# A two-layer streaming encoder: the first weight pieces taken tile by tile, another order of the first transfers, cache rows written from loaded tiles, and new keys

## The chip, the core and the metric

The kernel runs on one core of a Trainium2 chip, as one program. The metric is the device time of one execution in microseconds (us). The core has the engines PE (matmul; its weight loads are shown as PEld), DVE (VectorE), ACT (ScalarE), POOL (GpSimd) and SP, whose queue issues all transfers of this kernel. The transfers run on 16 DMA engines. Each engine takes its instructions in order; they wait for each other through semaphores.

## The reference

Two layers are computed over 1152 rows: 1024 frames of one new stream (eight tiles of 128 rows, tiles 0 to 7) and 16 frames of each of eight running streams (tile 8). All is in float32.

```python
xn = rms_norm(x, norm_mix)
q, k, v, u = split(xn @ w_in)                       # 512 | 128 | 128 | 512 columns
q, k = rope(rms_norm(q, q_gain)), rope(rms_norm(k, k_gain))
attn = sink_attention(q, keys, vals, sinks)         # 128 rows of window, 8 heads on 2 kv heads
pool = multi_scale_pool(u) @ w_pool * scale
x = x + concat(attn, pool) @ w_out                  # 1024 x 1024
h = rms_norm(x, norm_ffn) @ w_up                    # 1024 x 5632
c = conv_b + sum(h[t - 2 + j] * conv_w[j] for j in range(3))
x = x + (silu(c_gate) * c_val) @ w_down             # 2816 x 1024
```

For the running streams, keys and values are those of a cache of 128 rows followed by the 16 new ones. The newest 128 rows of keys and values are outputs: for these streams, rows 16 to 127 of the cache (outputs `nk_s` and `nv_s`, rows 0 to 111) and the 16 new rows.

## The kernel before

**Products.** A float32 product is made of three matmuls (`mm3`, lines 153 to 156) on operands that are split into a rounded part and the rest. A weight piece is loaded as 128 x 512 floats into a tile `raw` (five of them), and `w_split` makes the rounded part with a cast (line 182 on DVE, line 184 on ACT; the key `e_w` says how many of four consecutive pieces go to DVE) and the rest with a subtract (line 185, DVE), into a tile `W` (six of them, 512 KB each). The mixer goes through its weights three times, for three batches of three tiles. A piece with a key is stored after its split into DRAM (`wsd`, line 188; the profile calls these arrays wd0k, wd0u, wd0o and so on), and later batches load it from there (line 179) and don't split again. `w_advance` loads up to five pieces ahead and splits up to three ahead of the unit that is being written.

**A mixer layer.** For batch b, the stream `n` has the norms: for each tile `normA` (square and sum on ACT, line 255; a small scale on DVE, 256; the power on POOL, 257; the product with the gain on DVE, 258) and `normB` (eight transposes on PE, 278, a cast on ACT, 281, and a subtract on DVE, 282). `k0` to `k2` are the projections for q, k and v: eight pieces of 512 columns (one block of 128 rows each) and four of 256 columns (two blocks each), every one with three tiles. `u0` to `u2` make the pooling input, `p` the pooling product, `L` the attention of each tile step by step, `o` the output projection. `m0` to `m2` are the norms for the FFN.

**The hand-over to the FFN.** The FFN's up-projection uses seven products of sums (a Strassen-like scheme): `s0` and `s1` are twelve steps each, five splits (lines 314 on ACT and 315 on DVE), four additions (line 323) and others, for the first and the second half of the rows. `v` and `w` are the seven products of the first column pair for these halves; their results leave PSUM through ACT copies (line 932) or DVE additions (line 927). PSUM has four tiles `mm`, two `s` and two `tr`. The down-projection is also made of seven products, with five or four units each; `wt_load` fetches five and a half blocks of w_down that several products share, and `wd_load` the others.

**What sets the order.** The streams of a mixer layer are lists of tokens. A token has a key from `PLAN` (start and step for each stream, in no unit), tokens that must stand before it, and a few counts of buffers. `arrange` takes, again and again, the token of the smallest key that is allowed. This gives the order in which the program is written. From it the framework makes the order of each engine: it takes instructions by this order as a priority, but by its own model of time, so that instructions whose inputs are ready may pass others. Keys that begin with `e_` say which of ACT (0) or DVE (1) does a copy: `e_q`, `e_k`, `e_v` for the projections' results, `e_u` for the pooling input, `e_k2` for the keys, `e_pt0` and `e_pt1` for the transposed attention weights.

**The beginning.** `start` (lines 1328 to 1336) issues the first transfers: tile 0 of x, the identity, piece 0, the gain (a row broadcast to 128 partitions, 512 KB), piece 1, tiles 1 and 2, the other constants. In layer 0 the first norms are written as A, A, A, B, B, B (`wide` in `norms`), and `k0` follows when all three tiles are normed. `copies` (lines 1338 to 1342) moves the cache's rows 16 to 127 from DRAM to the outputs in DRAM, two transfers for each layer. `sample` loads the same caches into SBUF (lines 668 and 672) for the attention of tile 8.

Of the kernel before, what the change touches and what calls it, by code (L numbers as in the profile page):

```python
# [44 lines left out]
def arrange(tokens, limits):  # L45
# [19 lines left out]
PLAN = [  # L65
    dict(k0=(-17.62, 0.24), u0=(10.61, 1.71), k1=(30.79, 2.26), u1=(78.0, 4.62), o0=(92.76, 2.89), k2=(148.67, 0.53), u2=(167.09, 2.77), o1=(177.0, 4.18), o2=(235.82, 4.28), p0=(40.1, 4.11), p1=(87.53, 9.52), p2=(194.05, 11.9), n1=(-17.77, 3.16), n2=(24.42, 3.62), n3=(92.75, 0.67), m0=(218.99, 3.57), m1=(259.62, 0.1), m2=(181.18, 1.22), d=(4.13, 4.36), L=(26.9, 49.72, 64.52, 85.1, 108.8, 144.29, 159.45, 183.94, 209.44, 245.41), cw=(276.93, 6.24), sc=(242.61, 32.45), s0=(252.65, 2.67), s1=(279.21, 6.7), v=(236.08, 0.18), w=(265.61, 1.32), upw=(297.57, 0.58), e_q=0, e_k=1, e_v=1, e_u=0, e_k2=0, e_qt=0, e_pt0=0, e_pt1=1, e_ps0=1, e_ps1=1, e_ks=0, e_w=1, e_x0=0, e_x1=0, e_x2=1),
    dict(k0=(-52.3, 0.11), u0=(39.12, 0.62), k1=(27.74, 4.1), u1=(77.36, 4.61), o0=(81.16, 2.69), k2=(144.54, 0.53), u2=(154.52, 4.44), o1=(176.58, 5.19), o2=(244.07, 2.25), p0=(50.25, 5.11), p1=(72.82, 0.77), p2=(195.1, 13.29), n1=(-13.38, 2.12), n2=(30.2, 4.39), n3=(93.86, 2.01), m0=(219.6, 1.94), m1=(237.49, 1.8), m2=(278.02, 1.14), d=(-26.81, 5.35), L=(26.9, 49.72, 64.52, 87.91, 107.72, 142.58, 160.43, 180.13, 216.19, 239.71), cw=(266.26, 12.19), sc=(271.63, 4.65), s0=(264.1, 2.05), s1=(266.18, 3.7), v=(283.58, 0.14), w=(284.07, 11.47), upw=(287.29, 0.87), e_q=1, e_k=1, e_v=0, e_u=1, e_k2=0, e_qt=0, e_pt0=0, e_pt1=0, e_ps0=1, e_ps1=1, e_ks=0, e_w=1, e_x0=0, e_x1=1, e_x2=0),
]
# [3 lines left out]
def encoder_kernel(ctx: ExitStack, tc: tile.TileContext, consts, x_prompt, x_sample, cache_k, cache_v,  # L72
# [260 lines left out]
    def kvq_units(l, b):  # L333
        us = []
        for c, (cols, kn, n) in enumerate(((0, 1, 512), (512, 2, 256))):
            hold = {}
            for j in range(8 // kn):
                def f(w, c=c, kn=kn, n=n, j=j, hold=hold):
                    xT = state["xT", b]
                    wh, wl = [v.rearrange("p (k n) -> p k n", k=kn) for v in (w.hi, w.lo)]  # L340
                    for tl in range(3):
                        t = b * 3 + tl
                        if j == 0:
                            hold[tl] = P("mm")
                        o = hold[tl][:, 0:n]
# [4 lines left out]
                        if (j + 1) * kn == 8:  # L350
                            if c == 0:
                                state["qkv", t] = T("B", [128, 640])
                                copy(l, "e_q", state["qkv", t][:, 0:512], o)
                            else:
                                state["V", t] = T("V", [128, 128])
                                copy(l, "e_k", state["qkv", t][:, 512:640], o[:, 0:128])
                                copy(l, "e_v", state["V", t], o[:, 128:256])
                us.append(Unit(f, [in_piece(w_in[l], kn * j, cols, kn, n)]))
        return us
# [301 lines left out]
    def sample(l):  # L661
# [536 lines left out]
    def down_units(l):  # L1198
        us = []
        for u, (j, p) in enumerate(DSEQ):  # L1200
# [4 lines left out]
            def f(u=u, j=j, p=p, n=n, late=late, loads=loads, splits=splits):  # L1205
# [39 lines left out]
    def params1(l):  # L1245
        def f():
# [91 lines left out]
    def copies(l):  # L1338
        def f():
            sync.dma_start(out=nk_s[l, :, 0:112], in_=cache_k[l, :, 16:128])  # L1340
            sync.dma_start(out=nv_s[l, :, 0:112], in_=cache_v[l, :, 16:128])
        return f

    events = []
    pend = []
    for l in range(DEPTH):
# [160 lines left out]
```

## Time and profile before

| what | us |
|---|---|
| median of 3 runs | 2243.28 |
| lowest and highest | 2240.95, 2246.43 |
| the profiled execution | 2242.44 |
| its span, first to last instruction | 2240.7 |
| PE busy | 2169.5 (97%) |
| DVE busy | 1712.6 (76%) |
| ACT busy | 943.5 (42%) |

The mixer of layer 0 and its hand-over fill roughly the first 448 us, the FFN goes on to about 1120, the mixer of layer 1 and its hand-over to about 1520, and its FFN to the end. The mean granted clock of PE is 0.988. A row of a timeline has the start, the duration, the engine, the line, the operation with the tile it writes and the tiles it reads, and in brackets the idle time before it and what ended that. Busy time of PE counts matmuls up to modelled ends, so a busy PE can still run at a lower clock; the column with the granted clock shows that.

### The profile page before, as it was taken

The page shows a single profiled execution, that of the slowest core. Times are in us where ns is not written, and L with a number is a line of the kernel's source. Part 1 is how long each engine was busy: PE and PEld are TensorE (multiplying, and loading weights), DVE is VectorE, ACT ScalarE, POOL GpSimd, SP SyncE. Part 2 cuts the span into 40 slices and gives each one's busy share as a digit, 9 for nine tenths or more (in the row PEclk, how much of TensorE's full clock was granted, in tenths as well). Part 3 has the DMA queues.
Part 4 walks back from the last instruction along what each step waited for, and adds up shares of the span by engine and source line. Part 5 has one row for each costly group of instructions (what it writes and reads, how often), then busy time and mean ns, then how long its engine had stood idle before and what let it go on. Part 6 is the DMA issues. An engine that isn't in the chain of part 4 may idle for free.

```text
span 2240.7 us, 36002 instructions
## 1 busy us (share of the span) xinstructions
PE 2169.5 (97%) x13178; PEld 1945.5 (87%) x13178; DVE 1712.6 (76%) x3234; ACT 943.5 (42%) x1749; POOL 326.6 (15%) x499
## 2 busy tenths in 40 slices
PE   7999999899999999999999999979999999999999
PEld 6867777899999999878888887779999999988887
DVE  4776467989899998867557754689989999987663
ACT  3454345534343434443335543554343434353341
POOL 0000001121213232000000000111212233320000
PEclk9999999899999999999999999999999999999999
DMA  8757565122224346958765665532222343488663
GB/s 313 255 194 269 182 218 173 59 95 79 95 88 151 117 151 220 298 178 268 243 228 184 230 230 207 205 116 84 94 82 93 110 140 128 143 274 267 182 199 113
DMA packets 315940, 389.64 MB, mean 174 GB/s; under 512 B 21906, under 2 KB 219746, under 8 KB 315730
## 3 DMA queue, kind: packets, MB, share of 16 engines
q1 hardware_dynamic: 315762, 387.33, 52.2%
q8 instruction: 104, 1.70, 0.3%
q14 instruction: 74, 0.61, 0.1%
HBM read 279.71 MB, written 109.37 MB: 174 GB/s over the span
## 4 chain that ended last, share of the span: by engine, by line
PE 85%; DMA 6%; DVE 5%; ACT 2%; issue 1%; SPq 0%; POOL 0%; DVEq 0%; ACTq 0%
PE mm L154 15%; PE mm L155 15%; PE mm L156 15%; PE s L156 11%; PE s L154 11%; PE s L155 11%; PE s L644 2%; DMA raw<-in_w_down_dram 1%; DMA raw<-in_w_in_dram 1%; PE tr L631 1%; PE mm L448 1%; DMA W<-wd1o 1%; PE s L592 1%; DMA xd<-u 1%; PE tr L294 1%
## 5 line engine op out<-in xcount | busy, mean ns | idle before, releaser
L154 PE MATMUL mm<-B,W 128*128 128x288 f32 (+1 forms) x1376 | 422.1, 307 | 13.6 <-DVE B L927 7.7
L155 PE MATMUL mm<-B,W 128*128 128x288 f32 (+1 forms) x1376 | 419.2, 305 | 1.9 <-DVE B L315 1.8
L156 PE MATMUL mm<-B,W 128*128 128x288 f32 (+1 forms) x1376 | 417.2, 304 | 0.0
L154 PE MATMUL s<-B,B 128*128 128x512 f32 x704 | 279.6, 397 | 4.1 <-ACT B L1133 2.7
L156 PE MATMUL s<-B,B 128*128 128x512 f32 x704 | 279.2, 397 | 2.8 <-DVE B L1134 2.8
L155 PE MATMUL s<-B,B 128*128 128x512 f32 x704 | 278.6, 396 | 0.0
L154 PEld LDWEIGHTS mm<-B,W 128*128 128x128 f32 x1376 | 262.6, 191 | 17.9 <-DVE B L927 7.9
L155 PEld LDWEIGHTS mm<-B,W 128*128 128x128 f32 x1376 | 262.0, 190 | 3.4 <-DVE B L315 2.4
L156 PEld LDWEIGHTS mm<-B,W 128*128 128x128 f32 x1376 | 261.7, 190 | 1.0 <-DVE W L185 0.4
L975 DVE SCALAR_TENSOR_TENSOR B<-B,cvp,B 128x1168 f32<-128x1168 f32 x176 | 250.6, 1427 | 1.8 <-ACT B L973 1.5
L154 PE MATMUL mm<-W,B 128*128 128x512 f32 (+1 forms) x576 | 220.0, 388 | 12.4 <-ACT W L184 3.1
L155 PE MATMUL mm<-W,B 128*128 128x512 f32 (+1 forms) x576 | 214.8, 374 | 0.2 <-DVE W L185 0.2
L156 PE MATMUL mm<-W,B 128*128 128x512 f32 (+1 forms) x576 | 213.9, 374 | 0.0
L868 ACT CAST W<-Q 128x512 fp32r<-128x512 f32 x132 | 82.0, 621 | 258.1 <-PE mm L156 169.3
L1133 ACT CAST B<-B 128x256 fp32r<-128x256 f32 (+1 forms) x128 | 97.3, 780 | 204.7 <-DMA B<-gd 70.5
L154 PE MATMUL s<-B,W 128*128 128x288 f32 x576 | 171.2, 297 | 1.8 <-ACT B L314 1.2
L155 PE MATMUL s<-B,W 128*128 128x288 f32 x576 | 170.5, 296 | 0.0
L156 PE MATMUL s<-B,W 128*128 128x288 f32 x576 | 170.3, 296 | 0.0
L154 PEld LDWEIGHTS s<-B,B 128*128 128x128 f32 x704 | 133.2, 189 | 36.2 <-ACT B L1133 5.3
L156 PEld LDWEIGHTS s<-B,B 128*128 128x128 f32 x704 | 133.0, 189 | 34.9 <-DVE B L1134 3.6
L155 PEld LDWEIGHTS s<-B,B 128*128 128x128 f32 x704 | 133.1, 189 | 30.7
L869 DVE TENSOR_TENSOR W<-Q,W 128x512 fp32r<-128x512 f32 x132 | 134.6, 1020 | 20.6 <-ACT W L868 20.6
(236 smaller groups left out, 4855.8 us busy)
## 6 DMA issues: line engine op xcount, KB each, us to landing
raw<-in_w_up_dram SPq DMA_DIRECT2D x176, 256.0 KB
raw<-in_w_down_dram SPq DMA_DIRECT2D x154, 256.0 KB
gd<-B SPq DMA_DIRECT2D x44, 576.0 KB
B<-gd SPq DMA_DIRECT2D x32, 576.0 KB
W<-wd0o SPq DMA_DIRECT2D x32, 512.0 KB
W<-wd1o SPq DMA_DIRECT2D x32, 512.0 KB
W<-wd0k SPq DMA_DIRECT2D x24, 512.0 KB
W<-wd1k SPq DMA_DIRECT2D x24, 512.0 KB
```

What stands on the lines that cost most here:

```text
L154: pe.matmul(out=out, lhsT=a[0], rhs=b[0], start=first, stop=False)
L155: pe.matmul(out=out, lhsT=a[0], rhs=b[1], start=False, stop=False)
L156: pe.matmul(out=out, lhsT=a[1], rhs=b[0], start=False, stop=last)
L294: pe.transpose(out=tr[:, k * 128:(k + 1) * 128], in_=xn[:, c:c + 128], identity=ident)
L448: pe.matmul(out=o, lhsT=w.raw, rhs=d, start=True, stop=True)
L592: pe.matmul(out=p[:, i, kr], lhsT=q[:, h], rhs=K[:, g, kr], start=True, stop=False)
L631: pe.transpose(out=tr[:, h * 128:(h + 1) * 128], in_=S[:, h, kk * 128:(kk + 1) * 128], identity=ident)
L644: pe.matmul(out=o, lhsT=V, rhs=H.pop(("p", g, kk)), start=kk == kks[0], stop=kk == 1)
L868: act.copy(out=hi, in_=src)
L869: dve.tensor_tensor(out=lo, in0=src, in1=f32(hi), op=ALU.subtract)
L975: dve.scalar_tensor_tensor(out=c, in0=h[:, j:j + 1168], scalar=cvp[:, j, ct:ct + 1], in1=c, op0=ALU.mult, op1=ALU.add)
L1133: act.copy(out=h, in_=f32(o))
```

## The change

1. **Batch 0 of the projections** (`kvq_units`). The pieces 0, 1 and 2 of the 512 columns are no longer three units with three tiles each. They are three units with one tile each, which take all three pieces. The rest is as before. In batch 0, `k0.0` now waits for the norm of tile 0 only, `k0.1` for that of tile 1, `k0.2` for that of tile 2. In layer 0 the first norms are written A, B, A, B, A, B.
2. **Keys of pieces** (`keyed`). In layer 0 the pieces of `k0` have no key: they are not stored. Batch 1 loads the pieces raw again, splits them and stores them; batch 2 loads the stored ones.
3. **First transfers.** The order is now tile 0, identity, gain, piece 0, tile 1, pieces 1 and 2, tile 2, other constants.
4. **Cache rows.** `copies` is gone. Right behind the load of each cache into SBUF, its rows 16 to 127 are stored from the loaded tile.
5. **Shared blocks of w_down.** The six calls of `wt_load` are spread over units 2, 3 and 4 of the first product, two in each; they were one in each of units 0 to 3 and two in unit 4.
6. A small tile in `params1` has the tag V in place of D.
7. **Keys.** Both layers have new keys. Those that the prediction speaks of, start and step:

| stream | layer 0 before | layer 0 after | layer 1 before | layer 1 after |
|---|---|---|---|---|
| k0 | -17.62, 0.24 | 12.35, 0.15 | -52.3, 0.11 | -43.86, 0.15 |
| u0 | 10.61, 1.71 | 27.6, 1.13 | 39.12, 0.62 | 49.49, 0.1 |
| n2 | 24.42, 3.62 | 26.8, 3.63 | 30.2, 4.39 | 30.53, 4.46 |
| k1 | 30.79, 2.26 | 35.46, 2.26 | 27.74, 4.1 | 26.26, 4.1 |
| p1 | 87.53, 9.52 | 86.68, 12.45 | 72.82, 0.77 | 56.81, 4.29 |
| k2 | 148.67, 0.53 | 160.39, 1.54 | 144.54, 0.53 | 139.16, 1.11 |
| s0 | 252.65, 2.67 | 257.44, 3.18 | 264.1, 2.05 | 264.1, 2.08 |
| s1 | 279.21, 6.7 | 268.93, 2.61 | 266.18, 3.7 | 276.75, 4.45 |
| v | 236.08, 0.18 | 209.05, 0.65 | 283.58, 0.14 | 278.27, 0.1 |
| w | 265.61, 1.32 | 316.25, 1.16 | 284.07, 11.47 | 272.47, 516.37 |
| m2 | 181.18, 1.22 | 181.58, 0.95 | 278.02, 1.14 | 278.02, 1.14 |

In layer 0, `e_k`, `e_w` and `e_pt1` go from 1 to 0, and `e_u` and `e_k2` from 0 to 1. In layer 1, `e_q`, `e_k` and `e_u` go from 1 to 0 and `e_v` from 0 to 1.

```diff
-                def f(w, c=c, kn=kn, n=n, j=j, hold=hold):
...
+            def f(ws, js, tls, c=c, kn=kn, n=n, hold=hold):
+                xT = state["xT", b]
+                for tl in tls:
+                    t = b * 3 + tl
+                    if js[0] == 0:
+                        hold[tl] = P("mm")
+                    o = hold[tl][:, 0:n]
+                    for w, j in zip(ws, js):
...
+                            mm3(o, a, (wh[:, kk], wl[:, kk]), k == 0, k == 7)
...
+            ws = [in_piece(w_in[l], kn * j, cols, kn, n) for j in range(8 // kn)]
+            j0 = 0
+            if b == 0 and c == 0:
+                j0, first = 3, ws[0:3]
+                us.append(Unit(lambda *w, f=f: f(w, (0, 1, 2), [0]), first))
+                for tl in (1, 2):
+                    us.append(Unit(lambda f=f, tl=tl, first=first: f(first, (0, 1, 2), [tl])))
+            for j in range(j0, 8 // kn):
+                us.append(Unit(lambda w, f=f, j=j: f([w], [j], range(3)), [ws[j]]))
...
             H["ck"] = T("B", [128, 8, 128])
             sync.dma_start(out=H["ck"], in_=cache_k[l].rearrange("b t g d -> t b (g d)"))
+            sync.dma_start(out=nk_s[l, :, 0:112].rearrange("b t g d -> t b (g d)"), in_=H["ck"][16:128])
...
-                    for x in range(p, 6 if p == 4 else p + 1):
+                    for x in range(max(2 * p - 4, 0), max(2 * p - 2, 0)):
                         wt_load(l, x)
...
-            r = T("D", [4, 128])
+            r = T("V", [4, 128])
...
         x_load(0, [0])()
         sync.dma_start(out=cst[:, 0:C_M], in_=consts[:, 0:C_M])
+        gain_load(0, "n", norm_mix)()
         w_dma(order[0])
-        gain_load(0, "n", norm_mix)()
+        x_load(0, [1])()
         w_dma(order[1])
-        wptr["dma"] = 2
-        x_load(0, [1, 2])()
+        w_dma(order[2])
+        wptr["dma"] = 3
+        x_load(0, [2])()
...
+            if l == 0 and x == "k" and b == 0:
+                return units
+            for i, w in enumerate(w for u in units for w in u.ws):
+                w.key = l, x, i
...
-            wd = sn == "m2" or (sn == "n1" and l == 0)
+            wd = sn == "m2"
...
-        add("copy", pl["o1"][0], copies(l))
...
+            kpre = {0: [nn, f"k{b - 1}.11"], 11: ["par"]} if b else {0: ["n1.1"], 1: ["n1.3"], 2: ["n1.5"], 11: ["par"]}
```

More of the change, by code (lines that the diff above doesn't have):

```diff
@@ L67 @@
-    dict(k0=(-52.3, 0.11), u0=(39.12, 0.62), k1=(27.74, 4.1), u1=(77.36, 4.61), o0=(81.16, 2.69), k2=(144.54, 0.53), u2=(154.52, 4.44), o1=(176.58, 5.19), o2=(244.07, 2.25), p0=(50.25, 5.11), p1=(72.82, 0.77), p2=(195.1, 13.29), n1=(-13.38, 2.12), n2=(30.2, 4.39), n3=(93.86, 2.01), m0=(219.6, 1.94), m1=(237.49, 1.8), m2=(278.02, 1.14), d=(-26.81, 5.35), L=(26.9, 49.72, 64.52, 87.91, 107.72, 142.58, 160.43, 180.13, 216.19, 239.71), cw=(266.26, 12.19), sc=(271.63, 4.65), s0=(264.1, 2.05), s1=(266.18, 3.7), v=(283.58, 0.14), w=(284.07, 11.47), upw=(287.29, 0.87), e_q=1, e_k=1, e_v=0, e_u=1, e_k2=0, e_qt=0, e_pt0=0, e_pt1=0, e_ps0=1, e_ps1=1, e_ks=0, e_w=1, e_x0=0, e_x1=1, e_x2=0),
+    dict(k0=(12.35, 0.15), u0=(27.6, 1.13), k1=(35.46, 2.26), u1=(78.0, 4.62), o0=(92.76, 2.89), k2=(160.39, 1.54), u2=(167.47, 3.15), o1=(177.0, 4.09), o2=(235.74, 4.2), p0=(40.1, 3.5), p1=(86.68, 12.45), p2=(194.05, 11.9), n1=(-86.25, 2.26), n2=(26.8, 3.63), n3=(92.6, 1.1), m0=(218.99, 3.57), m1=(260.89, 0.13), m2=(181.58, 0.95), d=(-13.48, 3.86), L=(26.9, 49.72, 64.52, 85.45, 108.8, 144.29, 158.38, 183.7, 209.44, 245.41), cw=(259.88, 23.53), sc=(227.68, 60.94), s0=(257.44, 3.18), s1=(268.93, 2.61), v=(209.05, 0.65), w=(316.25, 1.16), upw=(342.36, 0.16), e_q=0, e_k=0, e_v=1, e_u=1, e_k2=1, e_qt=0, e_pt0=0, e_pt1=0, e_ps0=1, e_ps1=1, e_ks=0, e_w=0, e_x0=1, e_x1=0, e_x2=0),
@@ new lines @@
+    dict(k0=(-43.86, 0.15), u0=(49.49, 0.1), k1=(26.26, 4.1), u1=(76.32, 4.61), o0=(81.16, 2.69), k2=(139.16, 1.11), u2=(150.18, 5.15), o1=(175.45, 5.19), o2=(244.07, 2.25), p0=(49.92, 3.56), p1=(56.81, 4.29), p2=(193.02, 12.48), n1=(-18.93, 0.85), n2=(30.53, 4.46), n3=(92.15, 1.8), m0=(222.0, 1.72), m1=(234.28, 0.33), m2=(278.02, 1.14), d=(-24.93, 3.08), L=(26.9, 49.72, 64.52, 87.91, 106.15, 148.52, 158.51, 180.13, 216.19, 239.71), cw=(264.41, 12.12), sc=(273.99, 6.32), s0=(264.1, 2.08), s1=(276.75, 4.45), v=(278.27, 0.1), w=(272.47, 516.37), upw=(298.18, 0.41), e_q=0, e_k=0, e_v=1, e_u=0, e_k2=0, e_qt=0, e_pt0=0, e_pt1=0, e_ps0=1, e_ps1=1, e_ks=0, e_w=1, e_x0=0, e_x1=1, e_x2=0),
@@ L336, in kvq_units @@
             hold = {}
-            for j in range(8 // kn):
-                def f(w, c=c, kn=kn, n=n, j=j, hold=hold):
[L339 to L345, printed above, removed]
+            def f(ws, js, tls, c=c, kn=kn, n=n, hold=hold):
[6 more added lines that the diff above has]
+                    for w, j in zip(ws, js):
+                        wh, wl = [v.rearrange("p (k n) -> p k n", k=kn) for v in (w.hi, w.lo)]
                         for kk in range(kn):
@@ L349, in f @@
                             mm3(o, a, (wh[:, kk], wl[:, kk]), k == 0, k == 7)
[L350 to L358, printed above, removed]
+                    if (js[-1] + 1) * kn == 8:
+                        if c == 0:
+                            state["qkv", t] = T("B", [128, 640])
+                            copy(l, "e_q", state["qkv", t][:, 0:512], o)
+                        else:
+                            state["V", t] = T("V", [128, 128])
+                            copy(l, "e_k", state["qkv", t][:, 512:640], o[:, 0:128])
+                            copy(l, "e_v", state["V", t], o[:, 128:256])
+            ws = [in_piece(w_in[l], kn * j, cols, kn, n) for j in range(8 // kn)]
[7 more added lines that the diff above has]
+                us.append(Unit(lambda w, f=f, j=j: f([w], [j], range(3)), [ws[j]]))
         return us
@@ L672, in loadv @@
             sync.dma_start(out=H["cv"], in_=cache_v[l].rearrange("b t g d -> t b (g d)"))
+            sync.dma_start(out=nv_s[l, :, 0:112].rearrange("b t g d -> t b (g d)"), in_=H["cv"][16:128])
         def kc(i):
@@ L1357, in stream, with keyed @@
                 add(f"{st}.{i}", k + i * step, u, q, (res or {}).get(i))
-        def keyed(x, units, l=l):
-            for i, u in enumerate(units):
-                u.ws[0].key = l, x, i
+        def keyed(x, units, b, l=l):
+            if l == 0 and x == "k" and b == 0:
+                return units
+            for i, w in enumerate(w for u in units for w in u.ws):
+                w.key = l, x, i
             return units
@@ L1412, in encoder_kernel @@
         for b in range(3):
-            ou = keyed("o", out_units(l, b))
+            ou = keyed("o", out_units(l, b), b)
             pre = {0: [f"p{b}.3"], 4: [f"L.{lastidx[3 * b + 2]}"]}
```

10 lines of the change are left out of this document (2 added, 8 removed).

## The prediction

> **What bounds the kernel now.** I first read busy time by stretch, to see where the matmul engine is not full. The columns are the stretch, its length, and for each engine its busy time (instructions); last come the granted clock, the DMA share and GB/s.
>
> ```profile
> 0.00:60.00 60.00, 42.50 (x219) 36.79 (x220) 27.07 (x59) 20.00 (x38) 4.81 (x10) 0.96 0.87 317
> 60.00:168.00 108.00, 101.93 (x546) 83.31 (x546) 76.89 (x272) 56.49 (x156) 9.75 (x7) 0.96 0.62 218
> 392.00:448.00 56.00, 49.97 (x333) 48.68 (x334) 51.34 (x75) 28.83 (x38) 6.77 (x15) 0.88 0.19 59
> 448.00:1120.00 672.00, 668.34 (x4281) 623.24 (x4280) 562.10 (x868) 264.54 (x381) 124.99 (x203) 1.00 0.52 165
> 1440.00:1520.00 80.00, 67.76 (x400) 58.01 (x399) 61.00 (x81) 44.53 (x76) 9.64 (x13) 0.94 0.35 118
> ```
>
> The long FFN stretch is full (668.3 of 672). What an order can win lies elsewhere: 17.5 us without a matmul in the first 60, 6.1 up to 168, 6.0 and 12.2 where a mixer hands over to its FFN. So I read the first 60 us closely: the timeline (start, duration, engine, line; in brackets the idle before and its releaser), then the waits of PE (total, times, longest) over the whole run, with one row cut to the first 60 us, then finer stretches.
>
> ```profile
> 5.44 0.19 ACT L255 ACTIVATION_READ_ACCUMULATOR B<-B 128x1 f32 x1
> 7.25 0.43 DVE L182 CAST W<-raw 128x512 fp32r<-128x512 f32 x1 [2.30 <-DMA raw<-in_w_in_dram]
> 7.89 0.92 POOL L257 TENSOR_TENSOR st<-st,mhalf 128x1 f32<-128x1 f32 x1 [7.05 <-DVE st L256]
> 8.85 1.28 DVE L258 SCALAR_TENSOR_TENSOR B<-B,st,B 128x1024 f32<-128x1024 f32 x1 [0.45 <-POOL st L257]
> 10.19 1.54 PE L278 MATMUL tr<-cst,B 128*128 128x128 f32 x6 [10.19 <-DVE B L258]
> 11.90 1.06 ACT L255 ACTIVATE B<-B 128x1024 f32<-128x1024 f32 x1
> 12.95 0.46 ACT L281 CAST B<-tr 128x384 fp32r<-128x384 f32 x1
> 13.46 0.80 PE L154 MATMUL mm<-W,B 128*128 128x512 f32 x1 [1.74 <-ACT B L281]
> 17.53 0.63 PE L156 MATMUL mm<-W,B 128*128 128x512 f32 x1
> 17.95 0.52 PE L154 MATMUL mm<-W,B 128*128 128x512 f32 x1
> 18.31 0.49 PE L278 MATMUL tr<-cst,B 128*128 128x128 f32 x3
> 22.43 0.40 PE L154 MATMUL mm<-W,B 128*128 128x512 f32 x1
> 22.67 0.39 PE L155 MATMUL mm<-W,B 128*128 128x512 f32 x1
> 42.98 0.62 ACT L184 CAST W<-raw 128x512 fp32r<-128x512 f32 x1 [6.04 <-issue]
> ```
>
> ```profile
> PE mm L154 <- DVE B L927: 7.7, 1, 7.7
> PE s L156 <- DVE B L1134: 2.8, 2, 1.4
> PE s L154 <- ACT B L1133: 2.7, 2, 1.8
> PE mm L154 <- DMA W<-wd1o: 2.3, 3, 1.2
> ...
> PE tr L278 <- DVE B L258: 13.2, 2, 10.2
> PE mm L154 <- ACT W L184: 2.3, 1, 2.3
> ```
>
> ```profile
> 40.00:50.00 10.00, 7.44 (x42) 7.03 (x41) 4.18 (x11) 2.06 (x4) 0.00 (x0) 0.83 0.95 347
> 50.00:60.00 10.00, 6.98 (x40) 6.66 (x39) 5.68 (x14) 2.73 (x5) 2.48 (x2) 0.96 1.02 397
> 60.00:80.00 20.00, 20.00 (x115) 17.97 (x115) 16.34 (x67) 12.73 (x35) 2.61 (x3) 0.94 0.87 315
> 140.00:160.00 20.00, 15.39 (x65) 9.57 (x63) 12.93 (x50) 10.32 (x31) 1.39 (x2) 0.83 0.40 140
> ```
>
> The first matmul on weights stands at 13.46. Two stalls follow: 2.3 us on a weight cast that starts at 42.98, behind 6.04 us of ScalarE idle for which the profile has no releaser, and 3.0 us (13.2 less 10.2) on the norms of the second batch. Around them the DMA engines are full (0.95, 1.02) and the clock drops.
>
> **The change part by part.** The profiled execution took 2242.4 us (span 2240.7); the median of the runs shown, 2243.3, is 0.8 above it.
>
> *Start.* Piece 0's cast leaves VectorE for ScalarE (the key e_w), so L256 need not stand behind a raw piece that lands at 7.25: it can start when the square's sum is there, 5.44 + 0.19 = 5.63. From the end of that cast to L258, POOL's 0.92 included, the rows leave 8.85 − 7.25 − 0.43 = 1.2, so L258 could start at about 6.8 instead of 8.85, if its gain has landed. No row shows that landing; it is somewhere up to 8.85 with 256 KB of weights ahead of it, and those go behind it now. Ends 0 and 2.1; I take the middle, 1.0. Then the casts: the transposes end at 10.19 + 1.54 = 11.73, but the first cast starts at 12.95, behind the square of tile 2 at 11.90. With norms taken tile by tile that square is later in the order: 0 to 1.2, and I take 1.2, being a whole square. Together **−2.2**. Taking the three pieces tile by tile adds nothing of its own: PE's order is not the program's, and between 13.46 and 17.95 it already runs ten matmuls of tile 0 on pieces 0 to 3 before tile 1 is transposed at 18.31. That part I cost at nothing; what hides it is this reordering.
>
> *First weights.* The DMA issues say what leaves the first 60 us (KB each):
>
> ```profile
> wd0k<-W SPq DMA_DIRECT2D x12, 512.0 KB
> raw<-in_w_in_dram SPq DMA_DIRECT2D x40, 256.0 KB
> out_dram<-in_cache_k_dram SPq DMA_DIRECT2D x2, 448.0 KB
> out_dram<-in_cache_v_dram SPq DMA_DIRECT2D x2, 448.0 KB
> ```
>
> Twelve stores of split pieces are 6.3 MB; the four cache copies, issued at 22 to 30 us for both layers because nothing gates them, are 1.8 MB, each byte read and written. At 317 GB/s 60 us carry 19 MB, so a third or more goes. What this stretch can give is the two stalls (2.3 + 3.0) and the lost clock: 10 us at 0.83, 10 at 0.96, 20 at 0.94 are 1.7 + 0.4 + 1.2 = 3.3. Ends 0 and 8.6; nearest to full relief is the DMA row, but the 3.0 also had VectorE's order in it (pooling steps stood before the norm), so two thirds: **−5.7**. The Trainium skill, page "DMA: Bandwidth & Descriptors", section "Why a DMA increments its semaphore by 16 and not by 1", says a transfer is spread over the largest number up to 16 that divides its slowest dimension: by it the old copies (outermost 8 streams) sit on eight engines and the new stores (112 rows) on all sixteen, an estimate of twice the relief from the copies. No row here splits the engines, and my sum does without it.
>
> *Second batch.* The keyless pieces of batch 0 make batch 1 load raw, split and store: 12 times 256 + 512 KB in place of 512 KB, 3.1 MB more, and 12 casts and subtracts more.
>
> ```profile
> L185 DVE TENSOR_TENSOR W<-raw,W 128x512 fp32r<-128x512 f32 x72 | 48.9, 685 | 23.5 <-ACT W L184 23.1
> L184 ACT CAST W<-raw 128x512 fp32r<-128x512 f32 x55 | 34.1, 620 | 57.1 <-DMA raw<-in_w_in_dram 22.3 <-PE mm L156 17.9 <-issue 8.0
> L149 DVE COPY PT<-tr 128x512 f32<-128x512 f32 x16 | 10.9, 683 | 13.2 <-PE tr L631 13.2
> ```
>
> VectorE gets 12 × 0.685 = 8.2 us, ScalarE 7.4. In 60 to 80 VectorE has 16.3 of 20 us, so the cover is thin; over 60 to 168 it has 76.9 of 108. Other switches take some back: the 16 copies of attention weights (e_pt1) leave VectorE, 10.9 us over the layer. Ends 0 and +8.2; **+2**, nearer the row of 60 to 168.
>
> *Cache rows.* The two stores a layer now wait on SP for their own loads and stand before later weight loads there; both layers' copies used to be out of the way by 30 us. The nearest row is the wait for stored pieces in layer 1, 2.3 in all: ends 0 and +2.3, **+0.5**, since SP's order can put the store where the data has landed.
>
> *Hand-over to the FFN.* New keys put v ahead of m2's later steps in layer 1 and the sums s1 ahead of w in both (w.1 to w.6 last of all in layer 1). The place is the wait of 7.7:
>
> ```profile
> 1499.95 0.45 DVE L927 TENSOR_TENSOR B<-mm,PT 128x288 f32<-128x288 f32 x1
> 1500.46 0.61 PE L154 MATMUL mm<-B,W 128*128 128x288 f32 x1 [7.67 <-DVE B L927]
> L315 DVE TENSOR_TENSOR B<-B,B 128x1152 fp32r<-128x1152 f32 x28 | 37.5, 1352 | 6.0 <-ACT B L314 6.0
> ```
>
> PE waits there for a PSUM bank that one 0.45 us addition frees, queued on VectorE behind sums of 1.35 us each. Earlier v keys bring such additions forward, sums ahead of w push them back. What is late next is the first sum of s1, some microseconds on. Ends −7.7 and +7.7; **−1.5**, near zero as both act.
>
> *Deferred w_down blocks.* wt_load goes from down units 0 to 4 to units 2 to 4, so two loads of 512 KB less stand ahead of the first raw blocks on SP. The waits it could touch are 2.8 + 2.7 = 5.5 for both layers; against it, units 2 to 4 get two loads each. Ends −5.5 and +1.4 (one such wait more); **−0.5**, because these waits are released by splits, not by DMA.
>
> *All other keys* (u0, k2, p1, the DVE/ACT switches) move filler within mixers: I take 0, with ends of the size of one hole. 140 to 160 has 4.6 us idle and a clock of 0.83, which on 15.4 busy is 2.6 more: 7.2 either way. The scratch tile of params1 moving from D to V costs nothing, as V's five tiles are not in use that early.
>
> Sum: −2.2 − 5.7 + 2 + 0.5 − 1.5 − 0.5 = −7.4, so 2235.0 on the profiled execution and 2235.8 against the median. I say **2235**.
>
> **The rivals.**
> *Given back later, 2241.* PE comes out of the first 60 us earlier, but the attention of the first tiles (VectorE and ScalarE one after the other) sets when it gets on; then the hole at 140 to 160 grows by what was won. For: that hole is there now. Against: 60 to 140 is nearly full. Only the 1 to 2 us not lost there remain.
> *Hole healed, 2228.* The later u0 and k2 keys put matmuls where attention starves PE: the forecast less 7.2.
> *Start at half clock, 2238.* Matmuls of 512 columns start 0.42 us apart up to 17.95 and 0.24 apart at 22.43. Were the 27 matmuls of the three split units all that slow, not ten, 17 × 0.18 = 3.1 us of the start go back. Against: three batches of nine leave little room for a pause. The Trainium skill, "TensorE: Matmul & The Clock Gate", Part 1, says the half rate ends after some 3.4 us of sustained work, whatever its number of matmuls. By that rule warm-up moves with the start, unless the pieces come in drips; the trace agrees, with about 4.5 us from 13.46 to 17.95.
> *Slower, 2251: sums before additions.* If w's additions really queue behind all of s1, the 7.7 us wait stays in layer 1, comes a second time for w, and appears in layer 0: the forecast plus 1.5 (not won) plus 2 × 7.7 is 2251.9, rounded down. It decides when VectorE's first L927 after v starts later than the last L315 of s1. For: VectorE is busy 51.3 of 56 there. Against: six PSUM banks cover most of the sums.
>
> **How the numbers follow.** Chances: forecast 0.40 (own range 2229 to 2240), given back 0.22, hole healed 0.15, half clock 0.08, slower 0.15. About 0.3% is what a measurement of this kernel can tell from no change: 2236.6 and 2250.0 around the median. Faster: 0.26 of the forecast, 0.15 healed, 0.05 from the others, 0.46. Slower: most of that rival, 0.13. Same: 0.41. The range, 2222 to 2250, leaves out the far tail below the healed case and most of the slower one.
>
> **What would show it.** Right: first L154 near 11; no PE wait over 1 us in 40 to 60 and a clock near 1; the DMA share there well under 0.9; no 7.7 us wait at the second hand-over. Wrong: L258 still near 8.9, so the gain was the limit; a wider hole before 168; VectorE over 90% in 60 to 110 with PE waiting on L185; or a long L927 wait in both layers.

## The result, and the profile after

| kernel | median, us | lowest to highest | runs |
|---|---|---|---|
| before | 2242.11 | 2239.06 to 2246.43 | 4 |
| changed | 2227.06 | 2223.63 to 2228.42 | 4 |

The ratio is 0.9924, with an interval of 0.9908 to 0.994; the medians differ by 15 us. (Ratios here are those of the record. They are not the quotients of the medians beside them, which are higher or lower by up to 0.001.) The profiled execution took 2223.63 us, 18.8 less than the one before. It is the fastest of its four, so the profiles show a few us more than the medians.

The head of the page of the changed kernel (span, then busy time, share and instructions of each engine):

```profile
span 2221.8 us, 36068 instructions
...
PE 2157.7 (97%) x13178; PEld 1935.6 (87%) x13178; DVE 1705.8 (77%) x3210; ACT 966.2 (43%) x1797; POOL 326.8 (15%) x499
```

PE runs as many instructions as before (x13178 on both pages) in 11.8 us less busy time (2169.5 before). An order does not make a matmul shorter; a higher clock does. So a part of the gain is not in the idle time at all. The stretches of the changed kernel, in the columns of the prediction:

```profile
0.00:60.00 60.00, 47.50 (x260) 42.26 (x261) 36.27 (x77) 29.69 (x58) 4.48 (x10) 0.97 0.75 259
60.00:168.00 108.00, 100.86 (x545) 82.53 (x544) 82.41 (x274) 61.17 (x166) 10.95 (x7) 0.98 0.63 217
392.00:448.00 56.00, 54.48 (x407) 54.05 (x406) 51.98 (x87) 25.69 (x35) 8.29 (x21) 0.99 0.26 84
448.00:1120.00 672.00, 667.29 (x4246) 618.98 (x4245) 555.40 (x855) 265.15 (x386) 122.77 (x199) 1.00 0.50 162
1440.00:1520.00 80.00, 71.16 (x463) 64.61 (x462) 73.15 (x102) 44.69 (x70) 12.04 (x20) 0.96 0.33 111
...
40.00:50.00 10.00, 10.00 (x73) 10.00 (x72) 7.20 (x15) 4.09 (x9) 2.26 (x2) 1.00 0.92 327
50.00:60.00 10.00, 10.00 (x64) 9.89 (x63) 9.38 (x25) 5.62 (x12) 0.00 (x0) 1.00 0.87 300
60.00:80.00 20.00, 17.22 (x86) 14.24 (x85) 18.64 (x63) 10.80 (x34) 4.52 (x3) 0.91 0.53 188
140.00:160.00 20.00, 17.61 (x89) 13.05 (x88) 15.18 (x55) 13.33 (x37) 2.51 (x2) 1.00 0.63 213
```

Two stalls at 40 to 60 are gone, with the clock at 1.00; 60 to 80, full before, now has 2.8 us without a matmul and a clock of 0.91. The long FFN stretch is as it was.

Such rows can be added up. I cut both executions into slices of 2 us (1120 and 1110 rows). In each, **idle** is 2 less PE's busy time, and **lost clock** is the busy time by (1 less the granted clock). Span less idle less lost clock is 2148.4 before, 2149.7 after, and between 2146.0 and 2151.7 in the twelve kernels below. So the two sums account for the difference between before and changed to 1.3 us, and between any two of these kernels to some 6:

| stretch, us | before: idle + lost | after: idle + lost | difference |
|---|---|---|---|
| 0 to 20, start | 11.9 + 0.0 | 12.5 + 0.9 | +1.5 |
| 20 to 100 | 6.3 + 3.1 | 4.4 + 2.3 | -2.7 |
| 100 to 200 | 5.6 + 2.8 | 3.8 + 0.0 | -4.6 |
| 200 to 300 | 3.3 + 3.1 | 1.2 + 0.0 | -5.2 |
| 300 to 364 | 5.3 + 1.6 | 5.5 + 0.0 | -1.4 |
| 364 to 432, first hand-over | 6.7 + 5.2 | 6.8 + 3.0 | -2.1 |
| 860 to 1000 | 3.7 + 1.4 | 4.7 + 1.6 | +1.2 |
| 1170 to 1440, mixer of layer 1 | 8.4 + 0.0 | 9.6 + 0.0 | +1.2 |
| 1440 to 1520, second hand-over | 12.2 + 3.0 | 8.8 + 1.9 | -4.5 |
| 1900 to 2060 | 3.2 + 1.6 | 2.7 + 0.0 | -2.1 |
| the rest | 3.8 + 0.0 | 2.3 + 0.0 | -1.5 |
| whole | 70.5 + 21.8 | 62.4 + 9.7 | -20.2 |

Half of it, 9.8, came between 100 and 300 us, where the prediction had put 0. And 12.1 of the 20.2 is lost clock.

Two limits of this table. First, lost clock differs between executions without any other order: e8 below has, matmul by matmul, the order on PE of the changed kernel, but shows 13.5 us of lost clock in all where that shows 9.7, and 4.2 where that shows 1.9 from 1440 to 1520. So 2 us of clock in one stretch of one profile prove nothing. Second, at the start the column of the granted clock reads 1.00 while the matmuls are slow: they start some 0.42 us apart from 13.46 to 17.95 before and from 11.04 to 14.20 after, 0.23 apart later. At half rate these are 2.2 and 1.6 us that the table leaves out. Counting does without the column: the 60th matmul of lines 154 to 156 starts at 31.8 us before and at 33.4 after, the 150th at 48.7 and 45.8.

### The profile page after: what moved, and what is told of

The parts are those of the page before. It is cut to its first block, busy times and chain, and to the rows that moved or that the text cites. A ratio compares the mean times of both kernels' runs of the same rounds, so it can differ in the third digit from the quotient of the medians.

```text
span 2221.8 us, 36068 instructions
## 1 busy us (share of the span) xinstructions
PE 2157.7 (97%) x13178; PEld 1935.6 (87%) x13178; DVE 1705.8 (77%) x3210; ACT 966.2 (43%) x1797; POOL 326.8 (15%) x499
## 3 DMA queue, kind: packets, MB, share of 16 engines
q1 hardware_dynamic: 319858, 384.18, 52.3%
## 4 chain that ended last, share of the span: by engine, by line
PE 84%; DMA 6%; DVE 4%; ACT 2%; issue 2%; SPq 0%; POOL 0%; DVEq 0%; ACTq 0%; POOLq 0%
PE mm L154 15%; PE mm L156 15%; PE mm L155 15%; PE s L154 11%; PE s L156 11%; PE s L155 11%; PE s L653 2%; DMA B<-gd 1%; DMA raw<-in_w_down_dram 1%; PE tr L640 1%; DMA W<-wd0o 1%; PE tr L278 1%; PE mm L457 1%; PE s L601 1%; PE s L602 1%
## 5 line engine op out<-in xcount | busy, mean ns | idle before, releaser
L154 PE MATMUL mm<-B,W 128*128 128x288 f32 (+1 forms) x1376 | 419.7, 305 | 12.6 <-ACT B L314 10.7
L155 PE MATMUL s<-B,B 128*128 128x512 f32 x704 | 277.9, 395 | 0.0
L154 PE MATMUL mm<-W,B 128*128 128x512 f32 (+1 forms) x576 | 216.4, 383 | 11.8 <-ACT W L184 3.8
```

What stands on the lines that cost most here:

```text
L154: pe.matmul(out=out, lhsT=a[0], rhs=b[0], start=first, stop=False)
L155: pe.matmul(out=out, lhsT=a[0], rhs=b[1], start=False, stop=False)
```

## The experiments

My theory when the result was in: the new keys carry the gain, by holes that close in the mixer of layer 0 and at the second hand-over. The rival: the edits to the first 60 us carry it, tile by tile, fewer stores, no copies, another start. Each kernel below computes the full reference. Ratios are against the kernel before on the same chip.

| kernel | median, us | before, us | ratio | interval |
|---|---|---|---|---|
| e1: all edits, old keys | 2235.28 | 2240.46 | 0.9972 | 0.9961 to 0.9983 |
| e2: kernel before, new keys | 2227.69 | 2240.46 | 0.9939 | 0.9919 to 0.9959 |
| e3: batch 0 stored again | 2225.26 | 2240.46 | 0.9923 | 0.9905 to 0.9941 |
| e4: copies in DRAM again | 2227.67 | 2240.46 | 0.9933 | 0.9915 to 0.995 |
| e5: parameters later | 2229.91 | 2242.04 | 0.9945 | 0.9925 to 0.9966 |
| e9: new numbers, old switches | 2232.67 | 2242.04 | 0.9962 | 0.9949 to 0.9974 |
| e10: old numbers, new switches | 2232.28 | 2242.04 | 0.9953 | 0.9938 to 0.9967 |
| e11: four old keys, layer 1 | 2230.29 | 2242.04 | 0.9951 | 0.9933 to 0.9968 |
| e6: all old keys, layer 1 | 2230.24 | 2242.80 | 0.9944 | 0.9933 to 0.9956 |
| e7: old start | 2234.42 | 2242.80 | 0.9959 | 0.9945 to 0.9974 |
| e8: shared blocks as before | 2224.75 | 2242.80 | 0.9922 | 0.991 to 0.9935 |
| e12: old keys of k2 and u2, layer 0 | 2231.70 | 2242.80 | 0.9948 | 0.9935 to 0.9961 |

### Keys or edits

e1 is the changed kernel with both lines of `PLAN` from before; e2 is the kernel before with both new lines.

```diff
 PLAN = [   # e1, the second as well
-    dict(k0=(12.35, 0.15), u0=(27.6, 1.13), k1=(35.46, 2.26),
+    dict(k0=(-17.62, 0.24), u0=(10.61, 1.71), k1=(30.79, 2.26),
...
```

> The changed kernel with the keys and switches of before (both lines of PLAN), all other edits kept. Theory A (my prediction: the first transfers, the missing stores and the moved copies carry the gain): 6 to 9 us faster than before, PE idle plus lost clock in the first 100 us at least 5 below the 21 of before. Theory B (the keys carry it, by filling the holes of PE at 140 to 170 and 270 to 290 and at the hand-overs): 0 to 4 us faster, and these holes stand as before (about 7 and 6 us, hand-overs 11 and 15).

> The kernel before with only the new keys and switches (both lines of PLAN). Theory A: 0 to 3 us faster, or slower, since the parameter loads, whose key of 10 now lies ahead of k0, delay the first weights with nothing won. Theory B: 9 to 14 us faster; the holes at 140 to 170 and 270 to 290 shrink to 3 and 1 us and the second hand-over from 15 to about 10.

All edits without the keys give 0.28%; the keys without the edits give 0.61%, and the interval of e2 covers the changed kernel's 0.9924. **The keys carry most of it.** In the slices e1 has 15.5 us of idle and lost clock from 100 to 300 (14.8 before), e2 has 5.2 (5.0 in the changed kernel). The time of e1 lies between the two theories, its holes stand as theory B said. In the first 100 us it has 19.1 us of idle and lost clock, 2.2 below the 21.3 of before and not the 5 of theory A.

### The traffic of the first 60 us

e3 takes away the two lines that leave the pieces of batch 0 without a key, so they are stored at once and batch 1 loads them split. e4 puts the cache copies back as they were and takes the two stores from loaded tiles away.

```diff
-            if l == 0 and x == "k" and b == 0:      # e3
-                return units
...
+        add("copy", pl["o1"][0], copies(l))         # e4
```

> The changed kernel with keys on the pieces of the first batch again, so that it stores them and the second batch loads them split. Theory A: 3 to 6 us slower than the changed kernel (ratio to before 0.994 to 0.995), with weight waits at 30 to 60. Theory B: within 2 us of the changed kernel (0.9915 to 0.9935), as the 12 splits saved on VectorE in the second batch pay for the transfers.

> The changed kernel with the DRAM to DRAM copies of the cache rows in place of the stores from the loaded tiles. Theory A: 1 to 3 us slower than the changed kernel, with the four copies again issued in the first 40 us and weight pieces late behind them. Theory B: within 1.5 us of it.

Neither is told apart from the changed kernel by its time. From 20 to 60 us, e3, then e4, then e2, which has all stores and all copies:

```profile
20.00:60.00 40.00, 40.00 (x228) 36.21 (x227) 23.34 (x49) 17.31 (x38) 2.52 (x2) 0.94 0.98 365
```

```profile
20.00:60.00 40.00, 39.86 (x232) 36.09 (x231) 24.47 (x50) 19.43 (x41) 3.09 (x2) 0.97 0.86 302
```

```profile
20.00:60.00 40.00, 37.47 (x212) 33.24 (x210) 19.30 (x41) 16.18 (x36) 2.52 (x2) 0.96 0.98 366
```

With the DMA engines at 0.98, as full as ever, e3 keeps PE busy for all 40 us. So full DMA engines were not what held PE there. In e2 2.5 us of idle remain (5.6 before); e1, with the edits and the old keys, has no idle time from 40 to 60. So the edits alone close both stalls, and the keys alone a part. Which edit it is stays open: e3 and e4 put back one kind of traffic each, and no kernel has both back with the other edits in place. e3 also shows that loading raw again in batch 1 is not what opened 60 to 80: it does not load raw again, and waits 2.6 us there on a VectorE step of the attention:

```profile
PE tr L278 <- DVE st L618: 2.6, 1, 2.6
```

The changed kernel waits 2.1 us there on a VectorE subtract of the norm (L282). VectorE, busy 18.64 of 20 us in the changed kernel and 17.68 in e3, ends the wait in both.

### Two holes in the mixer of layer 0

The new keys are numbers (the order) and switches (VectorE or ScalarE). e9 has the new numbers with the old `e_` switches of both layers, e10 the reverse. (`e_x0` and `e_x2` among them are read by no line of the kernel.) e12 puts back two pairs of numbers alone.

```diff
-    e_k=0, e_u=1, e_k2=1, e_pt1=0, e_w=0, e_x0=1, e_x2=0     # e9, layer 0
+    e_k=1, e_u=0, e_k2=0, e_pt1=1, e_w=1, e_x0=0, e_x2=1
...
-    k2=(160.39, 1.54), u2=(167.47, 3.15)                     # e12, layer 0
+    k2=(148.67, 0.53), u2=(167.09, 2.77)
```

> The changed kernel with the switches of before (which of VectorE and ScalarE does each copy), and the new key numbers. Theory N (the numbers fill the holes): within 3 us of the changed kernel, idle plus lost clock from 100 to 300 near its 5, not near the 14 of before. Theory W (the switches do it, 10 us less on VectorE in layer 1 and the weight copies off it in layer 0): 6 to 10 us slower than the changed kernel and the holes are back. Both: the start loses about 1.6 us, as the first cast is on VectorE again, ahead of the norm.

> The changed kernel with the key numbers of before and the new switches. Theory N: about as the kernel with all old keys (2235, ratio 0.996 to 0.998), with some 14 us idle and lost clock from 100 to 300. Theory W: within 3 us of the changed kernel (0.992 to 0.994).

> The changed kernel with the old numbers of k2 and u2 in layer 0. If these two made the filler for the holes, idle plus lost clock from 100 to 300 rises from 5 to 10 or more and the kernel is 4 to 8 us slower. Rival: the holes are filled by the earlier streams (u0, n2, k1, p1), and the rise is under 3 us.

The waits of PE between 100 and 300 us (total, times, longest) tell two holes apart. Before:

```profile
PE tr L631 <- DVE B L621: 2.7, 1, 2.7
PE tr L735 <- DVE B L727: 1.8, 1, 1.8
```

The first, at 143.53, is a transpose of attention weights that waits for the normalised softmax; the second, at 276.64, is the same step in the attention of tile 8. Their lines are 640 and 630, 746 and 738 in the changed kernel and those made from it. There neither wait is left; the longest is

```profile
PE tr L565 <- ACT PT L151: 1.3, 1, 1.3
```

How the first hole closed stands in the timelines, before and in the changed kernel: the last scores that go into this softmax, its step on VectorE, the transposes.

```profile
135.46 0.28 PE L593 MATMUL s<-B,Q 128*128 128x256 f32 x1
143.13 1.13 DVE L621 TENSOR_SCALAR B<-B,st 128x256 f32<-128x256 f32 x4
143.53 1.35 PE L631 MATMUL tr<-cst,B 128*128 128x128 f32 x8 [2.68 <-DVE B L621]
```

```profile
129.60 0.29 PE L602 MATMUL s<-B,Q 128*128 128x256 f32 x1
138.53 1.14 DVE L630 TENSOR_SCALAR B<-B,st 128x256 f32<-128x256 f32 x4
139.07 1.09 PE L640 MATMUL tr<-cst,B 128*128 128x128 f32 x8
```

The softmax is not quicker: its step starts 7.7 us after the scores before, 8.9 in the changed kernel. But between these scores and the transposes PE's order now has 36 weight matmuls in place of 18, and these fill the time. The four kernels with this hole (before, e1, e9, e10) have 18, the ten without it 36. The second hole is filled likewise: weight matmuls run up to 274.9 before and up to 277.9 in the changed kernel, the step starts at 275.2 and 276.3.

The stretch of the second hole, before and in the changed kernel:

```profile
270.00:290.00 20.00, 16.71 (x79) 12.06 (x78) 12.68 (x31) 4.95 (x18) 0.00 (x0) 0.83 0.61 197
```

```profile
270.00:290.00 20.00, 18.78 (x104) 13.90 (x103) 15.69 (x46) 11.59 (x41) 1.96 (x1) 1.00 0.33 108
```

In e9 the first wait is back and the second is not; in e12 the second is back and the first is not (e9, then e12):

```profile
PE tr L640 <- DVE B L630: 2.7, 1, 2.7
...
PE tr L746 <- ACT B L747: 0.6, 1, 0.6
```

```profile
PE tr L746 <- DVE B L738: 1.8, 1, 1.8
```

| kernel | first hole's wait | second hole's wait | idle + lost, 100 to 300 |
|---|---|---|---|
| before | 2.7 | 1.8 | 14.8 |
| e1, old numbers, old switches | 2.7 | 1.8 | 15.5 |
| e10, old numbers, new switches | 2.7 | 1.7 | 13.5 |
| e9, new numbers, old switches | 2.7 | none | 10.3 |
| e12, old k2 and u2 only | none | 1.8 | 8.7 |
| changed | none | none | 5.0 |

The second hole goes with the numbers of k2 and u2: e12 changes nothing else. With these put back, 3.7 of the 9.8 come back here. The first hole needs new numbers and new switches together: with either alone it stays. Which switch it is was not tried, nor how it comes to move the scores in PE's order. In time e9 is 8 us above the changed kernel, as theory W said, and e10 lies between its two theories. The time of e12, about 5 us above the changed kernel's, has another 3.0 in the first hand-over (12.8 against 9.8), but 2.5 of that is clock. In the times the intervals of e10 and e12 just overlap the changed kernel's, that of e9 does not.

### The second hand-over

e11 gives layer 1 its old v, w, s0 and s1; e6 gives it its whole old line.

```diff
-    s0=(264.1, 2.08), s1=(276.75, 4.45), v=(278.27, 0.1), w=(272.47, 516.37)   # e11, layer 1
+    s0=(264.1, 2.05), s1=(266.18, 3.7), v=(283.58, 0.14), w=(284.07, 11.47)
```

> The changed kernel with the old numbers of s0, s1, v and w in layer 1 alone. If the order of these four made the second hand-over shorter (idle plus lost clock from 1440 to 1520: 15.6 before, 11.0 after), it is 15 or more again, with a wait for L927 of about 7.7, and the kernel is 4 to 5 us slower than the changed one (ratio 0.994 to 0.9955). If the switches of layer 1 or the earlier stages did it, it stays near 11 and the ratio near 0.993.

> The changed kernel with the layer 1 line of PLAN as before, layer 0 new. Layer 0's holes (100 to 300: 14 before, 5 after) stay healed; the second hand-over loses what its old order cost (4 to 5 us, with the 7.7 us wait for L927). If the two layers' lines add up: 4 to 6 us slower than the changed kernel (ratio 0.994 to 0.995). Rival: layer 1's line is worth nothing beyond noise, within 2 us of the changed kernel.

The waits of PE from 1440 to 1520 us, first of the changed kernel, then of e11 (L938 is what was L927):

```profile
PE mm L154 <- ACT B L314: 6.4, 3, 3.9
PE mm L155 <- DVE B L315: 1.6, 2, 1.3
```

```profile
PE mm L154 <- DVE B L938: 7.7, 1, 7.7
```

Four keys bring the wait of 7.7 back, with 12.3 us of idle time in the stretch (12.2 before, 8.8 changed). The same wait stands in the profiles of e1, e10 and e6, all with these four keys old, and in neither e2 nor e9. What is left in its place is the first sums of s1: 3.9 us on a split on ScalarE. The two ratios, 0.9951 and 0.9944, are alike: no more is seen of the whole line of layer 1 than of these four keys. Against the changed kernel that is 4 to 6 us, with intervals that just overlap its own. In the slices of this stretch it is 4.3 us in e11 and 5.3 in e6, but only the idle time follows the keys: it is 11.8 to 12.7 in the five kernels with the four old keys and 8.7 to 10.3 in the nine with the new ones, some 3 us. The lost clock is 1.6 to 3.3 with the old and 1.7 to 4.4 with the new.

### The start

In the changed kernel's timeline (SPq is SP issuing a transfer):

```profile
7.29 1.28 DVE L258 SCALAR_TENSOR_TENSOR B<-B,st,B 128x1024 f32<-128x1024 f32 x1 [1.56 <-DMA B<-in_norm_mix_dram]
8.63 1.54 PE L278 MATMUL tr<-cst,B 128*128 128x128 f32 x6 [8.63 <-DVE B L258]
9.31 4.90 SPq L1265 DMA_DIRECT2D snk<-in_attn_sinks_dram  x8
10.52 0.47 ACT L281 CAST B<-tr 128x384 fp32r<-128x384 f32 x1
11.04 0.80 PE L154 MATMUL mm<-W,B 128*128 128x512 f32 x1 [0.87 <-ACT B L281]
14.66 0.36 SPq L218 DMA_DIRECT2D raw<-in_w_in_dram  x1
17.48 0.62 ACT L184 CAST W<-raw 128x512 fp32r<-128x512 f32 x1 [2.30 <-DMA raw<-in_w_in_dram]
18.15 0.79 PE L154 MATMUL mm<-W,B 128*128 128x512 f32 x1 [3.00 <-ACT W L184]
```

The first matmul on weights is at 11.04 instead of 13.46. But the fourth raw piece is issued at 14.66, behind the small parameter loads of `params1`: their key is 10, and k0's is now 12.35 (it was -17.62). PE runs out of pieces and waits 3.0 us. e5 moves the parameters behind k0's first token; e7 puts the old order of first transfers back.

```diff
-            add("par", 10, params1(0))        # e5
+            add("par", 13.2, params1(0))
...
-        gain_load(0, "n", norm_mix)()         # e7
         w_dma(order[0])
+        gain_load(0, "n", norm_mix)()
-        x_load(0, [1])()
         w_dma(order[1])
-        w_dma(order[2])
-        wptr["dma"] = 3
-        x_load(0, [2])()
+        wptr["dma"] = 2
+        x_load(0, [1, 2])()
```

> The changed kernel with the parameter loads of layer 0 (key 10) given the key 13.2, so behind the first pieces of k0 (12.35 on). Theory P: the fourth piece was issued at 14.7 behind eleven small parameter loads, and PE stood 3.0 us for it at 18.2; with the pieces ahead the idle of the first 20 us falls from 12.5 to 9 to 10, and the kernel is 2 to 4 us faster than the changed one (ratio 0.990 to 0.9915). Rival: DMA latency or ScalarE's order holds the fourth piece in any case, or the parameters are late for the first attention: within 1.5 us of the changed kernel.

> The changed kernel with the old order of the first transfers. Theory D (the first 20 us are bound by the transfers as a whole, so what comes earlier makes something else late): idle and lost clock of the first 20 us stay at 12 to 14, and the time within 1.5 us of the changed kernel. Theory A (my start term): first matmul on weights back at 13, and 2 us slower.

In e5 the wait on the cast falls to 0.27, yet the first matmul comes later (at 12.20), since L258 waits longer for its gain (idle 2.69 us, to 8.44):

```profile
9.78 1.54 PE L278 MATMUL tr<-cst,B 128*128 128x128 f32 x6 [9.78 <-DVE B L258]
12.20 0.80 PE L154 MATMUL mm<-W,B 128*128 128x512 f32 x1 [0.89 <-ACT B L281]
16.91 0.50 PE L154 MATMUL mm<-W,B 128*128 128x512 f32 x1 [0.27 <-ACT W L184]
```

Idle and lost clock of the first 20 us are 12.4 in e5, 13.3 in e7, 13.4 in the changed kernel, 11.9 before. Which transfer comes first chooses where PE waits; the sum moves by 1.5. The 60th matmul of lines 154 to 156, at 33.4 in the changed kernel, comes at 33.9 in e5 and 34.9 in e7. In all eleven kernels with the new numbers it comes at 33.4 to 35.6, with the old ones at 31.8 (before), 32.5 (e1) and 32.9 (e10). So the new numbers cost the start something that the place of the parameter loads alone does not give back. e5's time is no better, against theory P; its profile has 13.0 and 13.4 us of idle and lost clock in the two hand-overs, against 9.8 and 10.7, nearly all of the difference clock.

e7 was a surprise to both theories. It costs 0.35% and its interval does not meet the changed kernel's, by 0.0005. Its first matmul on weights is at 11.65, not at 13. The sum of 13.3 leaves out slow matmuls there: up to 22.59 they start 0.42 us apart in the timeline. Its later loss is spread: 4.2 from 200 to 364, 3.3 in the mixer of layer 1, 3.8 from 1900 to 2060. The 3.3 is idle time and lies outside what the others show: 12.9 us in that mixer, 7.9 to 10.0 in the other 13 kernels. The order of PE's 13178 matmuls differs from the changed kernel's at the start, but also among the places 7962 to 8247, from 1373 to 1432 us, where the edit changes no line: as far as this shows, the framework's model of time carries a shift of the start through to orders far behind. The mixer of layer 1, first e7, then the changed kernel:

```profile
1170.00:1440.00 270.00, 257.11 (x1386) 208.92 (x1384) 161.59 (x515) 131.83 (x365) 18.99 (x15) 1.00 0.64 219
```

```profile
1170.00:1440.00 270.00, 260.42 (x1401) 210.64 (x1401) 161.34 (x512) 137.09 (x369) 18.27 (x16) 1.00 0.63 217
```

The old start is not slow by itself: e2 has it too and is not told apart from the changed kernel. Which displaced instruction costs what stays open.

### Shared blocks of w_down

```diff
-                    for x in range(max(2 * p - 4, 0), max(2 * p - 2, 0)):   # e8
+                    for x in range(p, 6 if p == 4 else p + 1):
```

> The changed kernel with the old times of the shared w_down loads. My term was 0.5 us with ends of 5.5 and -1.4; if it is right, within 1.5 us of the changed kernel, and idle plus lost clock around the two starts of the down-projection (860 to 1000 and 1900 to 2060) within 2 us of its 8.8. Rival: 3 to 5 us slower, with longer waits on the first g splits there.

0.9922 against 0.9924: no difference, and 9.0 us of idle and lost clock in the two stretches in both. With e3 it is as fast as the changed kernel; no kernel here is measurably faster than that.

## Why the prediction came out as it did

The time lies in the range, in the direction forecast, and the gain is twice the size. By its steps:

- **Start, -2.2; measured +1.5, and +1.6 at the 60th matmul.** The mechanism of the norm was right, the transfers were left out. The first cast follows the transposes by 10.52 - 8.63 - 1.54 = 0.35 us, and the first matmul is at 11.04, as "near 11" said. L258 stands at 7.29, ended by the gain's landing, between the 6.8 hoped for and 8.85. But I costed the norm's chain and not the queue on SP. k0's new key puts the parameter loads ahead of the fourth piece, and the 2.4 us won went into the wait of 3.0; e5, with these loads behind, shifts the wait and wins nothing. "Start at half clock" came in part: the pieces came in drips, and the wait of 3.0 put the clock at 0.50 behind it, for 0.9 us of lost clock up to 20 and 0.6 more up to 22, against the 3.1 of that rival:

```profile
16.00:18.00 2.00, 0.00 (x0) 0.00 (x0) 1.35 (x2) 0.52 (x1) 0.54 (x2) 0.96 0.95 370
18.00:20.00 2.00, 1.85 (x8) 1.67 (x8) 1.87 (x2) 0.48 (x2) 0.47 (x1) 0.50 1.02 381
20.00:22.00 2.00, 2.00 (x10) 1.60 (x9) 1.14 (x3) 0.65 (x3) 0.00 (x0) 0.69 1.01 390
```

- **First weights, -5.7, and second batch, +2.** At their places both were near. 40 to 60 gave back 5.6 us idle and, by the two rows, 1.3 + 0.3 of clock, 7.2 in all (the forecast had taken 1.7 + 0.4, by the whole 10 us and not by PE's busy time); 60 to 80 went from 1.2 of lost clock to 2.8 idle and 1.5 lost, 3.1 worse. "Given back later" happened in part, though at 60 to 80 and not at 140. The reason failed. The forecast hung on the DMA share falling well under 0.9; it is 0.92 and 0.87, and e3 has no idle time from 20 to 60 at 0.98. The new stall is VectorE's, but e3 shows it without the reload that I costed.
- **Cache rows, +0.5, and deferred w_down blocks, -0.5.** e4 and e8 show neither; terms of this size cannot be told from 0, as 0.2% of the time (4 us) is the least that these runs resolve.
- **Hand-over to the FFN, -1.5; measured -2.1 and -4.5.** The place and the mechanism were right for the second. The 2.1 of the first hand-over is all clock and cannot be put down to the keys: e1, with the old ones, has 8.9 us of idle and lost clock there, less than the changed kernel's 9.8. Of the 4.5, 3.4 is idle time; the 1.1 of clock is within what e8 shows by chance. e11 shows the second: the wait of 7.7 goes and 3.9 stays in its place at s1's first split. I took a value near zero because sums ahead of w could have pushed the additions back. They did not, and "slower, sums before additions" fell with that: neither L938 nor L943 heads the waits of the changed kernel in that stretch.
- **All other keys, 0; measured -9.8 between 100 and 300.** This is the step that failed. I wrote that they "move filler within mixers: I take 0, with ends of the size of one hole", priced one hole at 7.2 and gave its healing 0.15. Two holes healed, at 140 to 150 and at 274 to 284, of which I had read the first only. The rows of 270 to 290 were there to be read, as was the one cause of both: PE waits for a VectorE step of a softmax with too few weight matmuls to fill the time. The rival "hole healed" had this mechanism, and named k2, which fills the second hole. Its time, 2228, met the measured 2227 by luck, by another sum: the first 100 us gave 1.2 where the forecast under it had 5.9, and the holes and the second hand-over gave more.

## What to carry to other kernels

When new keys and structural edits come together, price the keys by every hole in the stages that they order, each with its releaser and its lost clock, before taking them at 0. To find what carries a gain, run the keys without the edits and the edits without the keys first; those two runs pointed past most of the story about transfers. In a program whose order is planned by a model of time, an edit at the start can change the order far behind it (e7, 0.35% slower), so one version's gain of that size says little of the edit itself. Compare lost clock over several profiles, since equal orders gave 9.7 and 13.5 us of it.

## What the runs showed of the hardware

**A hole costs its length, and often as much again in clock.** The hole at 143 us of the kernel before, in slices of 2 us (the number before the last two is the granted clock):

```profile
142.00:144.00 2.00, 0.47 (x4) 0.40 (x4) 2.00 (x9) 1.13 (x6) 0.00 (x0) 1.00 1.04 365
144.00:146.00 2.00, 0.88 (x6) 0.41 (x4) 1.97 (x10) 1.31 (x4) 0.00 (x0) 0.62 0.99 387
146.00:148.00 2.00, 1.65 (x4) 1.05 (x5) 1.49 (x4) 0.29 (x1) 0.00 (x0) 0.50 0.39 145
148.00:150.00 2.00, 2.00 (x8) 1.46 (x7) 0.00 (x0) 0.79 (x2) 0.00 (x0) 0.50 0.00 0
150.00:152.00 2.00, 2.00 (x9) 0.95 (x8) 0.00 (x0) 1.14 (x3) 0.00 (x0) 0.67 0.00 0
152.00:154.00 2.00, 1.72 (x12) 1.11 (x10) 1.28 (x2) 1.25 (x4) 0.00 (x0) 1.00 0.00 0
```

PE is busy again from 148, but at half rate up to about 151.3: the lost shares of these slices, 0.38 + 0.50 + 0.50 + 0.33, doubled and taken by 2 us, are 6.8 us. Over the whole run such times at half rate last 3.4, 6.8 or 10.2 us: before, ten such times of 54.6 us in all, or sixteen times 3.4; after, seven times 3.4. Nine fewer would be 15.3 us of clock if PE were busy throughout; it was not, and 12.1 were won. The Trainium skill, "TensorE: Matmul & The Clock Gate", Part 1, section "What's actually happening", says that the clock halves after an idle window of 3413 ns and that these windows run freely; the lengths agree with that, but the windows were not idle, as the next rows show.

**The clock followed how busy PE was in a window of 3.41 us, not the length of a gap.** In the kernel before PE stood still for 2.68 us up to 143.53, and the clock halved 1 us later. It halved at 277.6 too, where the longest gap is the 1.78 us of the second hole, but not behind a gap of 2.40 us up to 1483.22. In the traces all changes of the clock lie on a raster of 3.41 us, which starts elsewhere in each execution. Windows on this raster, before:

```profile
141.08:144.50 3.42, 0.97 (x8) 0.79 (x8) 3.42 (x15) 2.05 (x9) 0.00 (x0) 1.00 1.03 375
274.21:277.62 3.41, 1.42 (x8) 0.72 (x6) 2.04 (x6) 0.76 (x4) 0.00 (x0) 1.00 0.47 151
277.62:281.03 3.41, 2.70 (x6) 1.39 (x7) 1.05 (x1) 0.83 (x3) 0.00 (x0) 0.50 0.07 9
1479.10:1482.52 3.42, 1.72 (x13) 1.48 (x12) 3.42 (x6) 3.18 (x6) 0.89 (x1) 1.00 0.62 214
1482.52:1485.93 3.41, 2.71 (x20) 2.71 (x21) 3.09 (x6) 0.65 (x1) 3.41 (x3) 1.00 0.73 252
```

With PE busy for 0.97 or 1.42 us of a window the next one ran at half rate; with 1.72 it did not. Counted in all 14 kernels: of the windows at full rate, all 69 with PE busy for less than 0.45 of them were followed by half rate, and none of the 8790 with more than 0.57; half rate ended after every window that was busy for 0.83 of its length or more, and after no other. The Trainium skill, on the same page under "Why this matters for your kernels", asks for no gap over about 3 us; here 1.78 us was enough once.

**Small loads hold a queue as large ones do.** From 9.31 to 14.21 us SP is at the eight loads of L1265, one number to 16 partitions each. The issue of one takes 0.31 to 0.42 us, that of a weight piece of 256 KB, which stood behind them, 0.36. The rest of the 4.90 us is gaps between the eight, for which the rows name no cause.
